# An encoder layer on one core: the issue order of the opening norms, weight splits and constant loads, and the place of the residual loads

## The chip, the core and the metric

The kernel runs on 1 core of one Trainium2 chip. Time is the device time of one execution in microseconds (us); the number compared is the median of several executions. The core has five engines that each take their own list of instructions strictly in order: TensorE (PE in the profile, its weight loads PEld), VectorE (DVE), ScalarE (ACT), GpSimd (POOL) and SyncE (SP). An instruction that waits holds back everything behind it on its engine. SyncE and GpSimd here also issue DMA transfers, which 16 DMA engines carry out.

## The reference, cut to what matters

One pre-norm layer over x of 2048 frames by 1024 channels, all in float32. The change touches the first step (the norm) and the residual addition.

```
h = rmsnorm(x, norm_mix)                  # x * rsqrt(mean(x*x) + 1e-6) * gain
proj = h @ w_in                           # columns: conv, S5, attention, HGRN groups
y = four mixers on the column groups, each rms-normalised with a gain
x = x + y @ w_out                         # residual
h = rmsnorm(x, norm_ffn)
x = x + square(relu(h @ w_ff1)) @ w_ff2
```

## The kernel before, in words

The 2048 frames go through the first half of the layer in 4 blocks of 512 (`TB`), each block in 4 tiles of 128 frames. Every matrix product is made of three float32r products: both operands are split into a high part (rounded) and a low part (the rest), and high*high, high*low and low*high are added in PSUM (`mm3`, L509 to L512).

**A norm** (`norm` in `make_hT`, L481 to L489) takes one tile: SyncE loads `xt` (512 KB, L484, 2 buffers); ScalarE squares it and adds up each row into `ssx` (L486); VectorE makes mean + eps (`rsx`, L92); GpSimd raises it to the power -0.5 (L93); VectorE multiplies the tile by it and by the gain `g_mix` (L488). TensorE then transposes the tile in two halves of four 128x128 blocks into the one PSUM buffer `tr` (L501), ScalarE writes the high part `hh` (L505) and VectorE the low part `hl` (L506). The second half's transposes wait until `hl` of the first half has read the buffer.

**A weight unit** (`load_split`, L98 to L111) is a 256 KB load into `wr` (L102, 6 buffers), a high part `wh` by ScalarE (L105) and a low part `wl` by VectorE (L111), 9 buffers each. The first product of the kernel (`attn_in`, through `tm_tile`, L531) needs 8 units and goes tile by tile: 24 matmuls a tile, into one of two PSUM buffers `mm`, which ScalarE (`qk`, L741) and VectorE (`va`, L742) empty. The products after it (`proj_fm`, L518) take two units each, starting with the 9th.

**Constants.** About 16 small loads are issued by GpSimd (L146 to L199: the masks `mraw`, `bones`, gains, `sink`, `lbp`, the GLU weights `wgr`), and VectorE turns them into what the mixers need (`masks` L147, `nsink` L172, `lbm` L179 and so on). Then come 11 loads for `s5_setup` (L229 to L244, from `lam` over `ldt` to `db`); the first VectorE instruction that needs one of these is L223, `t<-ldt`, on the table of time steps.

**The order.** The program text is handed to a scheduler that keeps the data dependences, sets buffers and waits, and orders each engine's list by priority: `first(-4000)` puts the norm of block 0 ahead of all, `tc.high_priority()` lifts the weight units. Which row stands first on an engine is therefore only seen in the built program. GpSimd's loads use 8 completion counters in turn, so that a load there waits for the one eight before it.

**The residual** (`outp`, L1101 to L1113) loops over two halves of the 1024 output columns and 4 tiles: a product with 8 units of `w_out`, a load `xr` of x (L1109, 2 buffers), `xr = product + xr` on VectorE (L1111), and a store to `x1d` (L1112). Beside it `out_in` (L1058 to L1098) transposes the operands of the next block through the same `tr` buffer.

## Time and profile before

| | us |
|---|---|
| median of 3 runs (2293.31 to 2297.61) | 2293.39 |
| the profiled execution, whole | 2296.33 |
| the same, span of its trace | 2294.5 |
| TensorE busy | 2205.3 |
| VectorE busy | 1449.5 |
| ScalarE busy | 961.3 |
| GpSimd busy | 194.4 |

The profiled execution lies 2.94 us above the median, and 1.83 us of it are outside the span. TensorE is busy for 96% of the span, so what can be won lies in the remaining 89 us: the places where TensorE has nothing to do. The views read are the busy time by stretch, TensorE's waits, and the list of instructions in order of time around the longest of them.

### The profile page before, as it was taken

Reading aid. Unit: us, or ns where it says so; the run is one execution under the profiler, and the core shown is the slowest. Engines: PE = TensorE matmul, PEld = TensorE weight load, DVE = VectorE, ACT = ScalarE, POOL = GpSimd, SP = SyncE. Lnnn points to the kernel's source line nnn. Section 1 sums busy time; section 2 is a strip of 40 time slices with the busy share of each in tenths; the row PEclk is TensorE's granted clock in tenths of the full one; section 3 lists DMA queues with packets and bytes.
Section 4 is the critical chain, followed back from the end, with each engine's and each line's share of the span. In section 5 each row is a group of like instructions: output and inputs, shape, how many; then the busy total and the mean of one; then the engine's idle time right before and its main releaser. Section 6 shows DMA issues by size and latency. Waiting matters only on the chain.

```text
span 2294.5 us, 32511 instructions
## 1 busy us (share of the span) xinstructions
PE 2205.3 (96%) x11460; PEld 1755.9 (77%) x11460; DVE 1449.5 (63%) x3044; ACT 961.3 (42%) x1914; POOL 194.4 (8%) x251
## 2 busy tenths in 40 slices
PE   4999999999999999999999999999999999999899
PEld 3777777777777787777788878888878877888787
DVE  4796796797679664596666676555534455465343
ACT  3444325324433433465565565555533223223121
POOL 3112212112211210000000000000000010000000
PEclk9999999999999999999999999999999999999999
DMA  6333334333443457646667575554655587475544
GB/s 174 97 89 94 98 98 138 109 105 100 139 116 104 129 195 232 196 153 202 195 196 210 151 235 156 152 148 147 201 165 195 181 293 233 146 248 175 190 165 152
DMA packets 391476, 372.97 MB, mean 163 GB/s; under 512 B 30656, under 2 KB 305184, under 8 KB 391312
## 3 DMA queue, kind: packets, MB, share of 16 engines
q1 hardware_dynamic: 388976, 365.05, 51.7%
q0 software_dynamic: 2336, 5.84, 1.0%
q8 instruction: 90, 1.47, 0.3%
q14 instruction: 74, 0.61, 0.1%
HBM read 265.97 MB, written 103.82 MB: 161 GB/s over the span
## 4 chain that ended last, share of the span: by engine, by line
PE 42%; DMA 6%; DVE 3%; ACT 1%; issue 1%; SPq 0%; DVEq 0%; ACTq 0%
PE mm L1548 19%; PE mm L1363 13%; PE hx L1363 7%; DMA wr<-in_w_ff_dram 5%; PE mx L1363 3%; DVE st L1520 1%; DMA tr<-tb 1%; DMA sr<-as 1%; DVE wr L1217 1%; DVE wl L1208 0%; ACT wh L1207 0%; ACT st L1519 0%; DMA tq<-x1d 0%; DVE tp L1217 0%; DVE tb L1327 0%
## 5 line engine op out<-in xcount | busy, mean ns | idle before, releaser
L1548 PE MATMUL mm<-wh,st 128*128 128x512 f32 x1728 | 549.2, 395 | 13.8 <-DVE tq L1217 6.1
L1548 PEld LDWEIGHTS mm<-wh,st 128*128 128x128 f32 x1728 | 325.8, 189 | 92.3 <-issue 9.6
L1548 PE MATMUL mm<-wl,st 128*128 128x512 f32 x864 | 341.1, 395 | 0.2 <-DVE wl L1208 0.2
L1363 PE MATMUL mm<-tb,wh 128*128 128x512 f32 x1024 | 323.8, 397 | 4.0 <-ACT tp L1369 1.9
L1519 ACT ACTIVATE st<-sr 128x1024 fp32r<-128x1024 f32 x112 | 115.4, 1054 | 343.6 <-PE mm L1548 244.2
L1363 PEld LDWEIGHTS mm<-tb,wh 128*128 128x128 f32 x1024 | 190.9, 189 | 53.7 <-ACT tp L1382 5.4
L510 PE MATMUL mm<-wh,hh 128*128 128x512 f32 x512 | 212.4, 415 | 0.7 <-ACT hh L505 0.7
L512 PE MATMUL mm<-wh,hl 128*128 128x512 f32 x512 | 205.9, 402 | 0.0
L105 ACT ACTIVATE wh<-wr 128x512 fp32r<-128x512 f32 x224 | 138.2, 629 | 158.6 <-PE mm L511 113.8
L511 PE MATMUL mm<-wl,hh 128*128 128x512 f32 x512 | 204.6, 400 | 0.0
L1363 PE MATMUL mm<-tb,wl 128*128 128x512 f32 x512 | 202.4, 396 | 1.0 <-DVE wl L1208 1.0
L1207 ACT ACTIVATE wh<-wr 128x512 fp32r<-128x512 f32 x204 | 124.8, 627 | 176.1 <-DVE wr L1217 83.4
L1548 PEld LDWEIGHTS mm<-wl,st 128*128 128x128 f32 x864 | 162.8, 188 | 38.9 <-DVE wl L1208 0.9
L1520 DVE TENSOR_TENSOR st<-sr,st 128x1024 fp32r<-128x1024 f32 x112 | 134.5, 1221 | 70.6 <-ACT st L1519 70.5
L111 DVE TENSOR_TENSOR wl<-wr,wh 128x512 fp32r<-128x512 f32 x224 | 150.2, 690 | 35.8 <-ACT wh L105 34.7
L1363 PE MATMUL hx<-tb,wh 128*128 128x512 f32 x512 | 161.1, 394 | 0.0
L1208 DVE TENSOR_TENSOR wl<-wr,wh 128x512 fp32r<-128x512 f32 x204 | 136.6, 687 | 36.5 <-ACT wh L1207 30.2
L510 PE MATMUL mm<-hh,wh 128*128 128x512 f32 x384 | 159.4, 415 | 0.0
L512 PE MATMUL mm<-hh,wl 128*128 128x512 f32 x384 | 152.7, 398 | 0.0
L511 PE MATMUL mm<-hl,wh 128*128 128x512 f32 x384 | 152.3, 397 | 0.0
L1363 PEld LDWEIGHTS mm<-tb,wl 128*128 128x128 f32 x512 | 96.6, 189 | 23.7 <-DVE wl L1208 1.4
L510 PEld LDWEIGHTS mm<-wh,hh 128*128 128x128 f32 x512 | 98.6, 193 | 20.8 <-ACT hh L505 1.3
(412 smaller groups left out, 3617.1 us busy)
## 6 DMA issues: line engine op xcount, KB each, us to landing
wr<-in_w_ff_dram SPq DMA_DIRECT2D x304, 256.0 KB, 3.9
as<-tp SPq DMA_DIRECT2D x224, 256.0 KB, 2.7
sr<-as SPq DMA_DIRECT2D x112, 512.0 KB, 4.6
wr<-in_w_in_dram SPq DMA_DIRECT2D x160, 256.0 KB, 3.1
wr<-in_w_out_dram SPq DMA_DIRECT2D x64, 256.0 KB, 4.0
xt<-in_x_dram SPq DMA_DIRECT2D x16, 512.0 KB, 3.6
xr<-in_x_dram SPq DMA_DIRECT2D x32, 256.0 KB, 3.0
x1d<-xr SPq DMA_DIRECT2D x32, 256.0 KB, 2.5
```

The source lines that it names most:

```text
L105: S.activation(out=hi, in_=raw, func=AF.Copy)
L111: (G if le == "p" else V).tensor_tensor(out=lo, in0=raw, in1=hi, op=ALU.subtract)
L510: PE.matmul(ps, lhsT=lh, rhs=rh, start=first, stop=False)
L511: PE.matmul(ps, lhsT=lh, rhs=rl, start=False, stop=False)
L512: PE.matmul(ps, lhsT=ll, rhs=rh, start=False, stop=last)
L1207: S.activation(out=h, in_=raw, func=AF.Copy)
L1208: V.tensor_tensor(out=l, in0=raw, in1=h, op=ALU.subtract)
L1217: V.tensor_tensor(out=o, in0=x, in1=y, op=op)
L1363: PE.matmul(ps, lhsT=(wh, wl)[lw][:, ks], rhs=b[lb][:, k, :], start=first and k == 0 and q == 0, stop=k == 3 and q == 2, skip_group_check= ...
L1519: S.activation(out=s_[:, 0, ks], in_=r, func=AF.Copy)
L1520: V.tensor_tensor(out=s_[:, 1, ks], in0=r, in1=s_[:, 0, ks], op=ALU.subtract)
L1548: PE.matmul(ps, lhsT=st_[:, ls, k, :], rhs=tu[n, k][lt], start=k == 0 and p_ == 0, stop=k == NJ - 1 and p_ == 2)
```

## The change

It has three parts. (1) `make_hT` and the gain's load move up in the text, and the norm of block 0 is written there; `rstd_of` keeps each GpSimd power in a list `pows`, and each norm keeps its power and its scaling. (2) With `tc.issue_after(...)`, everything written inside the block is put behind the given instruction: all constant loads and their arithmetic behind the first norm's power, the loads of `s5_setup` behind the fourth norm's power, and the first step of `attn_in` of block 0 (its 8 weight units and the first matmuls) behind the first norm's scaling. (3) In `outp` the load of `xr` is written ahead of the product and made high priority. No arithmetic is changed.

```
@@ -86,11 +86,13 @@
+    pows = []
     def rstd_of(pool, ss, n, inv, tag):
...
-        G.tensor_tensor(out=r, in0=r, in1=mhalf[:, 0:n], op=ALU.pow)
+        pows.append(G.tensor_tensor(out=r, in0=r, in1=mhalf[:, 0:n], op=ALU.pow).ins)
@@ -141,15 +143,62 @@
+    g_mix = c1.tile([P, D], F32, tag="gain", name="g_mix")
+    with first(-3998):
+        SY.dma_start(out=g_mix, in_=a["norm_mix"].partition_broadcast(P))
+    norms = []
+    def make_hT(b):
...
+            i_ = V.scalar_tensor_tensor(out=xt, in0=xt, scalar=r, in1=g_mix, op0=ALU.mult, op1=ALU.mult)
+            norms.append((pows[-1], i_.ins))
+            return xt
...
+    with first(-4000):
+        run(make_hT(0))
+    after = tc.issue_after(norms[0][0])
+    after.__enter__()
     masks = cm.tile([P, 4, P], U8, name="masks")
     mraw = mix.tile([P, 4, P], F32, tag="cva0", name="mraw")
     G.dma_start(out=mraw, in_=a["c_masks"])
...
@@ -200,6 +249,7 @@
         V.tensor_tensor(out=wgl[:, c], in0=wr, in1=wgh[:, c], op=ALU.subtract)
+    after.__exit__(None, None, None)
@@ -1103,20 +1122,15 @@
             for i in range(4):
-                ps = yield from tm_tile(ws, i)
                 xr = c1.tile([P, 512], F32, tag="xr", name="xr", bufs=2)
                 t0 = b * TB + i * P
-                SY.dma_start(out=xr, in_=a["x"][t0:t0 + P, ns])
+                with tc.high_priority():
+                    SY.dma_start(out=xr, in_=a["x"][t0:t0 + P, ns])
+                ps = yield from tm_tile(ws, i)
@@ -1147,13 +1161,16 @@
-    with first(-4000):
-        run(make_hT(0))
     s5p = None
     setup = s5_setup()
-    next(setup)
+    with tc.issue_after(norms[3][0]):
+        next(setup)
     for b in range(NB):
-        dense(attn_in(b))
+        g = attn_in(b)
+        if b == 0:
+            with tc.issue_after(norms[0][1]):
+                next(g)
+        dense(g)
```

The built programs differ in few rows: in the opening of all five engines, and around the residual on SyncE and VectorE. Line numbers in the rows of the changed kernel are its own.

**First norms.** VectorE, from its first row that waits for anything. Before:

```order
L147 CAST masks<-mraw 128x512
L92 TENSOR_SCALAR rsx<-ssx 128x1
L111 TENSOR_TENSOR wl<-wr,wh 128x512 x7
L488 SCALAR_TENSOR_TENSOR xt<-xt,rsx,g_mix 128x1024
L111 TENSOR_TENSOR wl<-wr,wh 128x512
L92 TENSOR_SCALAR rsx<-ssx 128x1
L111 TENSOR_TENSOR wl<-wr,wh 128x512
L488 SCALAR_TENSOR_TENSOR xt<-xt,rsx,g_mix 128x1024
L506 TENSOR_TENSOR hl<-tr,hh 128x4x128
```

Now:

```order
L94 TENSOR_SCALAR rsx<-ssx 128x1
L168 SCALAR_TENSOR_TENSOR xt<-xt,rsx,g_mix 128x1024
L94 TENSOR_SCALAR rsx<-ssx 128x1
L113 TENSOR_TENSOR wl<-wr,wh 128x512 x2
L168 SCALAR_TENSOR_TENSOR xt<-xt,rsx,g_mix 128x1024
L187 TENSOR_TENSOR hl<-tr,hh 128x4x128
L113 TENSOR_TENSOR wl<-wr,wh 128x512 x3
L187 TENSOR_TENSOR hl<-tr,hh 128x4x128
L113 TENSOR_TENSOR wl<-wr,wh 128x512 x3
L187 TENSOR_TENSOR hl<-tr,hh 128x4x128
```

The cast of the masks is gone from the head (it now stands behind the low part of the second tile's first half), the first scaling stands ahead of all weight splits, and the splits come in groups of 2, 3 and 3 between the norm's pieces.

GpSimd at the same place; `ISA` is a configuration instruction, the TENSOR_TENSOR rows are the norms' powers. Before (behind ten constant loads that begin with `mraw`):

```order
L168 DMA sink<-in_attn_sinks_dram 64x2x1
L93 ISA
L93 TENSOR_TENSOR rsx<-rsx,mhalf 128x1
L168 DMA sink<-in_attn_sinks_dram 64x2x1
L174 DMA ogain<-in_hg_out_norm_dram 128x64
L177 DMA lbp<-in_hg_lower_bounds_dram 128x2x1
L199 DMA wgr<-in_s_w_glu_dram 128x512
L93 TENSOR_TENSOR rsx<-rsx,mhalf 128x1
L199 DMA wgr<-in_s_w_glu_dram 128x512
L229 DMA lam<-in_s_lam_re_dram 8x128
```

Now, from the first row of the program proper:

```order
L95 ISA
L95 TENSOR_TENSOR rsx<-rsx,mhalf 128x1
L198 DMA mraw<-in_c_masks_dram 128x512
L201 DMA bones<-in_c_bones_dram 128x2
L203 DMA g_grp<-in_group_norm_dram 128x768
L95 TENSOR_TENSOR rsx<-rsx,mhalf 128x1
L205 DMA g_grpa<-in_group_norm_dram 128x2x1
```

The first power stands ahead of every load and the second behind three; the rest of the constants follow up to both `wgr`, then the third and the fourth power, and only then `lam` and the other loads of `s5_setup`.

**End of the opening.** VectorE around `t<-ldt`; `qss`, `qrs`, `qn` belong to the attention of the first tile. Before, with the third tile's `hl` as the last row:

```order
L742 COPY va<-mm 128x128
L223 TENSOR_SCALAR t_783<-ldt 128x8
L217 TENSOR_TENSOR db<-db,ident 16x256
L766 TENSOR_REDUCE qss<-qsq 128x6
L221 TENSOR_SCALAR t_784<-t_783 128x8
L92 TENSOR_SCALAR qrs<-qss 128x6
L221 TENSOR_SCALAR t_784<-t_784 128x8
L506 TENSOR_TENSOR hl<-tr,hh 128x4x128
```

Now, ending with the `va` of the third tile, which frees a PSUM buffer:

```order
L789 TENSOR_TENSOR qn<-qk,qrs 128x2x2x64
L187 TENSOR_TENSOR hl<-tr,hh 128x4x128
L793 TENSOR_TENSOR qn<-qk,qrs 128x128
L168 SCALAR_TENSOR_TENSOR xt<-xt,rsx,g_mix 128x1024
L273 TENSOR_SCALAR t_783<-ldt 128x8
L267 TENSOR_TENSOR db<-db,ident 16x256
L271 TENSOR_SCALAR t_784<-t_783 128x8
L271 TENSOR_SCALAR t_784<-t_784 128x8
L761 COPY va<-mm 128x128
```

All eight `hl` of block 0 now stand ahead of `t<-ldt` (the last of them is seen here), and behind it come the third tile's `va` and, further on, the low parts of the weight units from the 10th.

**Residual.** SyncE in the second block's turn; `x1d` rows are the stores, `w_out` rows the weight units of the next half. Before:

```order
L1109 DMA xr<-in_x_dram 128x512
L1112 DMA x1d_64<-xr 128x512
L102 DMA wr<-in_w_out_dram 128x512 x8
L1112 DMA x1d_64<-xr 128x512
L1109 DMA xr<-in_x_dram 128x512 x2
L1112 DMA x1d_64<-xr 128x512
L1071 DMA ybt<-ybd_76 128x256
L1072 DMA ybt<-ycdd_79 128x512
L1109 DMA xr<-in_x_dram 128x512
```

Now:

```order
L1128 DMA xr<-in_x_dram 128x512
L1132 DMA x1d_64<-xr 128x512
L104 DMA wr<-in_w_out_dram 128x512 x3
L1128 DMA xr<-in_x_dram 128x512
L104 DMA wr<-in_w_out_dram 128x512 x5
L1132 DMA x1d_64<-xr 128x512 x2
L1128 DMA xr<-in_x_dram 128x512 x2
```

The first `xr` of the new half stands behind three of the eight weight loads instead of behind all eight. The same is found in the third block's turn, and in the first block's with three of six.

## Rows read from the trace of the kernel before

**Rows 1.** The page: the span, the busy times of the engines with their share and instruction count, the group of VectorE's weight splits (busy in all, mean ns of one, idle before), and two DMA groups over the whole span (count, KB each, median us from issue to landing).

```profile
span 2294.5 us, 32511 instructions
...
PE 2205.3 (96%) x11460; PEld 1755.9 (77%) x11460; DVE 1449.5 (63%) x3044; ACT 961.3 (42%) x1914; POOL 194.4 (8%) x251
...
L111 DVE TENSOR_TENSOR wl<-wr,wh 128x512 fp32r<-128x512 f32 x224 | 150.2, 690 | 35.8 <-ACT wh L105 34.7
...
xr<-in_x_dram SPq DMA_DIRECT2D x32, 256.0 KB, 3.0
x1d<-xr SPq DMA_DIRECT2D x32, 256.0 KB, 2.5
```

**Rows 2.** Busy time by stretch, late in the opening and behind it: from:to, length, then PE, PEld, DVE, ACT and POOL busy (instructions), granted clock of TensorE, DMA share, GB/s.

```profile
40.00:60.00 20.00, 15.34 (x66) 12.63 (x67) 11.82 (x36) 8.51 (x16) 2.98 (x4) 0.83 0.24 82
60.00:100.00 40.00, 40.00 (x213) 32.14 (x212) 25.75 (x69) 16.62 (x45) 7.04 (x6) 1.00 0.44 122
```

**Rows 3.** TensorE's waits over the whole span: who waited for whom, us in all, times, the longest.

```profile
PE tr L501 <- DVE xt L488: 21.9, 1, 21.9
PE tr L501 <- DVE hl L506: 8.5, 3, 7.6
PE tr L1093 <- DVE hl L1098: 6.8, 4, 3.0
```

**Rows 4.** Instructions in order of time, from the first constant load to the end of the first tile: start, duration, engine, line, what, and the idle time before it with its releaser.

```profile
1.26 0.68 POOL L146 DMA_DIRECT2D mraw<-in_c_masks_dram  x1 [0.81 <-POOLq L1578]
...
1.67 0.42 SPq L152 DMA_DIRECT2D g_mix<-in_norm_mix_dram  x1
...
4.32 1.06 ACT L486 ACTIVATE junk<-xt 128x1024 bf16<-128x1024 f32 x1 [2.30 <-DMA xt<-in_x_dram]
...
7.37 0.43 DVE L147 CAST masks<-mraw 128x512 uint8<-128x512 f32 x1 [5.76 <-DMA mraw<-in_c_masks_dram]
...
10.62 0.60 POOL L168 DMA_DIRECT2D sink<-in_attn_sinks_dram  x1 [1.95 <-DMA g_grp<-in_group_norm_dram]
11.33 0.59 POOL L93 TENSOR_TENSOR rsx<-rsx,mhalf 128x1 f32<-128x1 f32 x1
...
13.06 0.72 POOL L177 DMA_DIRECT2D lbp<-in_hg_lower_bounds_dram  x1
...
14.56 2.43 ACT L105 ACTIVATE wh<-wr 128x512 fp32r<-128x512 f32 x4 [1.22 <-DMA wr<-in_w_in_dram]
...
20.56 1.28 DVE L488 SCALAR_TENSOR_TENSOR xt<-xt,rsx,g_mix 128x1024 f32<-128x1024 f32 x1
...
21.75 0.68 DVE L111 TENSOR_TENSOR wl<-wr,wh 128x512 fp32r<-128x512 f32 x1
...
21.89 1.11 PE L501 MATMUL tr<-ident,xt 128*128 128x128 f32 x4 [21.89 <-DVE xt L488]
...
33.53 0.49 ACT L741 ACTIVATE qk<-mm 128x384 f32<-128x384 f32 x1 [0.79 <-PE mm L512]
```

**Rows 5.** DMA issues of the first 60 us: count, KB each, median us from issue to landing.

```profile
xt<-in_x_dram SPq DMA_DIRECT2D x6, 512.0 KB, 3.6
g_mix<-in_norm_mix_dram SPq DMA_DIRECT2D x1, 512.0 KB, 7.7
...
lbp<-in_hg_lower_bounds_dram POOLq DMA_DIRECT2D x1, 1.0 KB, 5.0
```

**Rows 6.** In order of time: GpSimd's issue of the first load of the S5 setup and of the two loads of `ldt`, and SyncE's issue of the fourth tile.

```profile
24.07 0.55 POOL L229 DMA_DIRECT2D lam<-in_s_lam_re_dram  x1
...
29.81 1.39 POOL L240 DMA_DIRECT2D ldt<-in_s_log_dt_dram  x2
...
32.14 0.33 SPq L484 DMA_DIRECT2D xt<-in_x_dram  x1
```

**Rows 7.** In order of time: VectorE's first instruction on `ldt`, what stands around it, and TensorE up to the first product behind `attn_in`.

```profile
42.71 0.17 DVE L223 TENSOR_SCALAR t<-ldt 128x8 f32<-128x8 f32 x1 [7.81 <-DMA ldt<-in_s_log_dt_dram]
...
43.94 1.06 ACT L486 ACTIVATE junk<-xt 128x1024 bf16<-128x1024 f32 x1 [7.89 <-DMA xt<-in_x_dram]
...
44.66 1.11 PE L501 MATMUL tr<-ident,xt 128*128 128x128 f32 x4 [7.62 <-DVE hl L506]
...
61.80 0.39 PE L510 MATMUL mm<-hh,wh 128*128 128x512 f32 x1
```

**Rows 8.** In order of time: SyncE, VectorE and TensorE around the first `xr` of the second half in the second block's turn.

```profile
869.76 0.32 SPq L1112 DMA_DIRECT2D x1d<-xr  x1
...
870.74 5.67 SPq L102 DMA_DIRECT2D wr<-in_w_out_dram  x8
...
876.93 4.23 SPq L1109 DMA_DIRECT2D xr<-in_x_dram  x2
...
881.53 0.69 DVE L1111 TENSOR_TENSOR xr<-mm,xr 128x512 f32<-128x512 f32 x1 [5.15 <-DMA xr<-in_x_dram]
...
882.75 0.55 PE L1093 MATMUL tr<-ident,ybt 128*128 128x128 f32 x3 [2.98 <-DVE hl L1098]
```

**Rows 9.** The same in the third block's turn.

```profile
930.29 0.69 DVE L1111 TENSOR_TENSOR xr<-mm,xr 128x512 f32<-128x512 f32 x1 [5.20 <-DMA xr<-in_x_dram]
...
931.50 0.55 PE L1093 MATMUL tr<-ident,ybt 128*128 128x128 f32 x3 [2.00 <-DVE hl L1098]
```

**Rows 10.** Busy time of the 8 us behind that, in the columns of rows 2.

```profile
932.00:940.00 8.00, 8.00 (x36) 6.46 (x34) 2.30 (x5) 1.74 (x5) 0.00 (x0) 0.79 0.41 140
```

More of the change, by code (lines that the diff above doesn't have):

```diff
@@ L143, in emit, with run, norm @@
     junks = {k: cm.tile([P, GW], BF16, name="junk" + k) for k in "chg"}
+    g_mix = c1.tile([P, D], F32, tag="gain", name="g_mix")
+    with first(-3998):
+        SY.dma_start(out=g_mix, in_=a["norm_mix"].partition_broadcast(P))
+    def run(g):
+        r = None
+        for r in g:
+            pass
+        return r
+    norms = []
+    def make_hT(b):
+        def norm(i):
+            t0 = b * TB + i * P
+            xt = big.tile([P, D], F32, tag="xt", name="xt", bufs=2)
+            SY.dma_start(out=xt, in_=a["x"][t0:t0 + P, :])
+            ss = mix.tile([P, 1], F32, tag="ssx", name="ssx", bufs=2)
+            S.activation(out=junk, in_=xt, func=AF.Square, accum_out=ss)
+            r = rstd_of(mix, ss, 1, 1.0 / D, "rsx")
+            i_ = V.scalar_tensor_tensor(out=xt, in0=xt, scalar=r, in1=g_mix, op0=ALU.mult, op1=ALU.mult)
+            norms.append((pows[-1], i_.ins))
+            return xt
+        nx = norm(0)
+        yield
+        for i in range(4):
+            xt = nx
+            if i < 3:
+                nx = norm(i + 1)
+            for k4 in range(2):
+                pt = psum_tr()
+                for k in range(4):
+                    kk = k4 * 4 + k
+                    PE.transpose(pt[:, k * P:(k + 1) * P], xt[:, kk * P:(kk + 1) * P], ident)
+                pv = pt.rearrange("p (k t) -> p k t", k=4)
+                oh = hh[:, k4 * 4:k4 * 4 + 4, i * P:(i + 1) * P]
+                ol = hl[:, k4 * 4:k4 * 4 + 4, i * P:(i + 1) * P]
+                S.activation(out=oh, in_=pv, func=AF.Copy)
+                V.tensor_tensor(out=ol, in0=pv, in1=oh, op=ALU.subtract)
+                yield
+    with first(-4000):
+        run(make_hT(0))
+    after = tc.issue_after(norms[0][0])
+    after.__enter__()
     masks = cm.tile([P, 4, P], U8, name="masks")
@@ L149, in emit @@
     G.dma_start(out=bones, in_=a["c_bones"])
-    g_mix = c1.tile([P, D], F32, tag="gain", name="g_mix")
-    with first(-3998):
-        SY.dma_start(out=g_mix, in_=a["norm_mix"].partition_broadcast(P))
     g_grp = cm.tile([P, 3 * GW], F32, name="g_grp")
@@ L475, in s5_setup @@
                 SY.dma_start(out=two_d[:, gp, 2:4, :], in_=wsb)
-                yield
-    def make_hT(b):
-        def norm(i):
-            t0 = b * TB + i * P
-            xt = big.tile([P, D], F32, tag="xt", name="xt", bufs=2)
-            SY.dma_start(out=xt, in_=a["x"][t0:t0 + P, :])
-            ss = mix.tile([P, 1], F32, tag="ssx", name="ssx", bufs=2)
-            S.activation(out=junk, in_=xt, func=AF.Square, accum_out=ss)
-            r = rstd_of(mix, ss, 1, 1.0 / D, "rsx")
-            V.scalar_tensor_tensor(out=xt, in0=xt, scalar=r, in1=g_mix, op0=ALU.mult, op1=ALU.mult)
-            return xt
-        nx = norm(0)
-        yield
-        for i in range(4):
-            xt = nx
-            if i < 3:
-                nx = norm(i + 1)
-            for k4 in range(2):
-                pt = psum_tr()
-                for k in range(4):
-                    kk = k4 * 4 + k
-                    PE.transpose(pt[:, k * P:(k + 1) * P], xt[:, kk * P:(kk + 1) * P], ident)
-                pv = pt.rearrange("p (k t) -> p k t", k=4)
-                oh = hh[:, k4 * 4:k4 * 4 + 4, i * P:(i + 1) * P]
-                ol = hl[:, k4 * 4:k4 * 4 + 4, i * P:(i + 1) * P]
-                S.activation(out=oh, in_=pv, func=AF.Copy)
-                V.tensor_tensor(out=ol, in0=pv, in1=oh, op=ALU.subtract)
                 yield
@@ L1113, in outp @@
                 yield True
-    def run(g):
-        r = None
-        for r in g:
-            pass
-        return r
     tracks = []
```

## The prediction

> **What bounds the kernel now.** TensorE is busy for 2205.3 of 2294.5 us [rows 1]. An edit that only reorders work can win from the 89 us in which it stands, so the first view to read is TensorE's waits. One wait leads it by far: 21.9 us at the start, for the first scaled tile. Two more lie where the change reaches: 8.5 us in three waits for a norm's low part, one of them 7.6 us, and 6.8 us in four waits for the low part in `out_in` [rows 3]. The second view is the order of time around each, and there the question is what the engine that is named was itself waiting for.
>
> At the start VectorE holds the tile back, but not because it has work. The squares are done at 5.4 us; VectorE then stands at the cast of the masks until that load has landed, at 7.37. GpSimd, which has to raise to a power, is issuing constant loads and waits for one of them until 10.62; its power runs at 11.33 and is done at 11.9. By then VectorE stands in front of seven weight splits, and the first weights are not there before 14.56. The scaling runs at 20.56, the first transposes at 21.89, and the first tile is done at 33.53 [rows 4]. So two queues, not two computations, cost about 13 us.
>
> At 42.71 the same happens again: VectorE waits 7.81 us for `ldt`, a load of the S5 setup that nobody needs yet, and the third tile's low part is behind it; TensorE waits 7.62 us for that and starts at 44.66. The fourth tile, issued at 32.14, is there only at 43.94, 11.8 us later where 3.6 is the median [rows 5 to 7]; the two loads of `ldt` were moving in between. The first product behind `attn_in` begins at 61.80 [rows 7], and from there TensorE has no gap: 40.00 of 40 us [rows 2]. That makes 61.80 the mark to measure the opening by: what comes earlier there comes earlier at the end, since behind it the lists of all engines are the same up to the residual.
>
> **The change part by part: the first norm.** Removed from the path: the cast and the wait for its load, and the ten loads ahead of the power. The squares end at 5.4; two small steps, VectorE's (0.17, as in rows 7) and GpSimd's 0.59, give 6.3. The scaling also needs the gain: issued at 1.67, 7.7 to land, that is 9.4 [rows 4, 5]. That was with 640 KB of masks and gains on the same DMA engines; a 512 KB tile alone took 3.6, so the bounds are 6.3 and 9.4. I take 7.5, since the constants now come behind. Scaling 1.28: the first transposes at about 8.9 instead of 21.89. This is no gain of 13 us by itself, because the first tile's products need all eight weight units. Before, the eighth split ran at 21.75 [rows 4]; its loads are two buffers ahead at most, so I leave it at 20 to 22. The first tile is then done at about 22.5 instead of 33.5: eleven us at this point.
>
> The first power carries a risk that a page names: the Trainium skill, GPSIMD Engine Reference, section Instruction dispatch, says that the first call to a freshly loaded GpSimd kernel pays an instruction load of about 6 us that no row shows. The trace speaks against it: the first power ran at 11.33, 0.11 us after the load issue in front of it ended. By that page the sum would be some 6 us smaller in the opening; it is a rival below.
>
> **The third and fourth norm: what is late next.** The constants moved behind the first power. VectorE now has `nsink` and `lbm`, which need `sink` and `lbp`, ahead of the third scaling. Before, `lbp` was issued at 13.06 and took 5.0: landed at 18.1, 16.8 us after the first constant was issued at 1.26 [rows 4, 5]. The same train now starts at 6.4, so `lbp` lands at 23.2. Without it the third scaling could run at about 20.6 (transposes of the first tile done at 15, load 3.6, square 1.2, power 0.7). I take 23.3; the bounds are 20.6 and 28, the latter if the train is slowed by 5 us by the weights it now shares the engines with.
>
> From there VectorE's list up to the fourth norm's power holds the scaling (1.28), five full-width steps (0.69 each, the mean of the weight splits [rows 1]: 3.45), two halvings of the GLU weights (estimate 0.5 each, half the operands of a split) and about eight small ones (0.17: 1.4), 7.1 us; the power 0.6. So `lam`, the first load of the S5 setup, is issued at 31 instead of 24.07 [rows 6], with bounds 28 and 36. From `lam` to `ldt` landed it was 18.6 us (24.07 to 42.71) [rows 6, 7]: GpSimd's issue of eleven loads and the slow `ldt` itself, both unchanged. **So `ldt` lands at 49.6**, 7 us later than before.
>
> What waits for it has changed. All low parts of block 0 are now ahead of it. TensorE gets the fourth tile at about 32 to 33.4, has some two tiles of products left (24 matmuls each, about 5 us by the 213 in 40 us of rows 2) and is through at about 45. Then it needs a PSUM buffer, and the `va` that frees it is behind `ldt` on VectorE: 49.6 and four short steps, 50.8. The mark thus moves from 61.80 to 50.8: 11.0 us earlier. Two things come off. The second half of that product needs the tenth unit's low part, which has nine small steps (1.5), a norm's steps (0.2, 0.6, 1.28) and itself (0.69) ahead of it: 55.0, where TensorE arrives at 53.3; with VectorE's steps overlapping I take 1.5. And the pause of 6 us lies ahead of dense work: behind the pause of 7.6 the granted clock of the stretch was 0.83 [rows 2], so 3.4 of 20 us were lost at the lower level; about 1 us more than before. **Opening: -11.0 + 1.5 + 1.0 = -8.5 us**, bounds -3.5 (`lam` at 36) and -12 (`lam` at 28, no clock loss).
>
> **The residual loads.** In the second block's turn VectorE stood 5.15 us at the residual addition, from 876.4 to 881.53, for an `xr` issued at 876.93 behind eight weight loads, and the low part for TensorE was behind it: TensorE waited 2.98 [rows 8]. In the third block's turn it was 5.20 and 2.00 [rows 9]. Now `xr` goes out behind three of the eight: at 870.74 plus three eighths of 5.67, 872.9. Its buffer was stored from 869.76, 2.5 to land: free at 872.3. It takes 3.0 to 4.6 and is there at 876 to 877.5; VectorE then reaches the low part as soon as ScalarE's high part is there. Both of TensorE's waits go: **-5.0 us**. Bounds: -1, if another wait of VectorE takes the place; -6.7, since behind the second one the clock was 0.79 for 8 us [rows 10], 1.7 us lost. The other loads that move by one or two rows cost nothing: two 256 KB issues of 0.4 us each, in front of weights that VectorE paces.
>
> **Sum.** -8.5 - 5.0 = -13.5. On the profiled execution 2296.3 becomes 2282.8; it lay 2.9 above the median, and 2293.4 becomes **2279.9**, say 2280.0.
>
> **The rivals.** *The residual loads bring nothing* (VectorE waits for the product or a weight split there instead; against it: its wait was for the DMA alone, and TensorE's product was done): -8.5, 2285.0. Chance 0.13. *The first power pays a start cost of its own*, by the rule of the page cited: constants, `lam` and `ldt` 6 us later, opening -2.5, in all -7.5, 2286. Against it the 0.11 us. Chance 0.08. *The S5 loads take back the opening*: the third norm's constants, or the eight counters of GpSimd's loads, hold the fourth power until `lam` goes out at 38 to 40; then `ldt` lands at 57 to 59, the mark is at 59 to 61, and what is left is about half of the residual's gain: 2291, no change. For it: each of these loads took 5 us and more when weights ran beside it. Chance 0.11. *Slower: an `xr` load holds the weights.* It stands in the middle of `w_out` loads, and SyncE waits there until the buffer is free. If that buffer is the one stored at 876.46 and not at 869.76, five weight loads are held until about 879, 6 us in each of three turns, and TensorE needs them in the next half: +18 against -8.5, 2303. It decides itself by whether SyncE idles over 2 us behind the third weight load. Against it: before, the first `xr` went out right behind the store issue, with no wait. Chance 0.08.
>
> **How the numbers follow.** My forecast has 0.55, a larger gain (under 2272, if `ldt` is no longer the last to come) 0.05. About 0.2% of this kernel, 4.6 us, can be told from no change: faster is under 2288.8. Faster: 0.55 + 0.05 + 0.13 + 0.08 = 0.81; same 0.11; slower 0.08. The forecast's own bounds are 2274.7 to 2288.9. The range leaves out the slower rival, half of the no-change one and the larger gain, under 2 in 10: 2272.0 to 2290.0.
>
> **What would show it.** First transposes at 8 to 11 us; first tile done at 20 to 24; `lam` issued at 28 to 36; VectorE waiting for `ldt` with the low parts ahead of it, until 47 to 55; the first product behind `attn_in` at 49 to 58; in the residual no wait of VectorE for `xr` over 1 us and TensorE's wait for the `out_in` low part down from 6.8 to about 2. I am wrong if a constant that I let land by 23 is there only after 30, or if a later wait grows by what the opening wins: TensorE's waits behind 61.80 must stay what they are.

## The result, and the profile after

| | us |
|---|---|
| before, on the same chip: median of 4 runs (2293.31 to 2297.61) | 2294.63 |
| after: median of 4 runs (2280.79 to 2284.63) | 2281.13 |
| ratio after to before, with its 95% interval | 0.9943 (0.9927 to 0.9959) |
| profiled execution of after, span | 2282.9 |

The change makes the kernel 0.57% faster: 13.1 us by the ratio, where 13.5 were forecast. Line numbers below are those of the changed kernel, unless a row of before is named.

The first views are the page and TensorE's waits over the span; they answer to [rows 1] and [rows 3].

```profile
span 2282.9 us, 32514 instructions
...
PE 2205.5 (97%) x11460; PEld 1755.1 (77%) x11460; DVE 1447.6 (63%) x3044; ACT 959.6 (42%) x1914; POOL 194.7 (9%) x251
```

```profile
PE tr L182 <- DVE xt L168: 8.4, 1, 8.4
...
PE tr L182 <- DVE hl L187: 6.4, 2, 6.0
...
PE mm L529 <- DVE va L761: 4.2, 1, 4.2
```

TensorE's busy time is that of before to 0.2 us; the gain is idle time alone. The wait for the first scaled tile fell from 21.9 to 8.4 us, and the wait for a low part from 8.5 to 6.4. A new one stands where the prediction put it: 4.2 us for `va`, behind `ldt`.

The opening in order of time, which answers to [rows 4, 6, 7]: start, duration, engine, line, what, and the idle time ahead with its releaser.

```profile
5.80 0.56 POOL L95 TENSOR_TENSOR rsx<-rsx,mhalf 128x1 f32<-128x1 f32 x1 [5.35 <-DVE rsx L94]
7.09 1.28 DVE L168 SCALAR_TENSOR_TENSOR xt<-xt,rsx,g_mix 128x1024 f32<-128x1024 f32 x1 [1.38 <-DMA g_mix<-in_norm_mix_dram]
8.43 1.11 PE L182 MATMUL tr<-ident,xt 128*128 128x128 f32 x4 [8.43 <-DVE xt L168]
16.58 0.71 POOL L226 DMA_DIRECT2D lbp<-in_hg_lower_bounds_dram  x1
25.85 0.16 DVE L228 TENSOR_TENSOR lbm<-lbp 128x2 f32<-128x2 f32 x1 [4.02 <-DMA lbp<-in_hg_lower_bounds_dram]
25.93 1.28 DVE L168 SCALAR_TENSOR_TENSOR xt<-xt,rsx,g_mix 128x1024 f32<-128x1024 f32 x1
26.63 0.48 ACT L760 ACTIVATE qk<-mm 128x384 f32<-128x384 f32 x1
32.53 0.58 POOL L279 DMA_DIRECT2D lam<-in_s_lam_re_dram  x1
38.24 1.38 POOL L290 DMA_DIRECT2D ldt<-in_s_log_dt_dram  x2
38.80 0.34 SPq L164 DMA_DIRECT2D xt<-in_x_dram  x1
47.45 1.06 ACT L166 ACTIVATE junk<-xt 128x1024 bf16<-128x1024 f32 x1 [5.20 <-DMA xt<-in_x_dram]
50.38 0.17 DVE L273 TENSOR_SCALAR t<-ldt 128x8 f32<-128x8 f32 x1 [6.37 <-DMA ldt<-in_s_log_dt_dram]
51.08 0.28 DVE L761 COPY va<-mm 128x128 f32<-128x128 f32 x1
51.41 0.80 PE L529 MATMUL mm<-hh,wh 128*128 128x512 f32 x1 [4.25 <-DVE va L761]
```

The chain of the prediction is all there: the third scaling stands behind `lbp`, `lam` behind the fourth norm's power, the first product behind `attn_in` (the mark) behind `ldt` and `va`. The mark went from 61.80 to 51.41.

The residual in the second block's turn, which answers to [rows 8]:

```profile
861.46 1.53 SPq L104 DMA_DIRECT2D wr<-in_w_out_dram  x3
863.08 0.38 SPq L1128 DMA_DIRECT2D xr<-in_x_dram  x1
863.56 3.71 SPq L104 DMA_DIRECT2D wr<-in_w_out_dram  x5
867.31 3.28 SPq L1132 DMA_DIRECT2D x1d<-xr  x2
873.37 0.95 SPq L1128 DMA_DIRECT2D xr<-in_x_dram  x2
```

```profile
864.36 0.69 DVE L1131 TENSOR_TENSOR xr<-mm,xr 128x512 f32<-128x512 f32 x1
869.55 0.69 DVE L1131 TENSOR_TENSOR xr<-mm,xr 128x512 f32<-128x512 f32 x1 [2.30 <-PE mm L530]
...
876.13 0.69 DVE L1131 TENSOR_TENSOR xr<-mm,xr 128x512 f32<-128x512 f32 x1 [3.67 <-DMA xr<-in_x_dram]
...
900.02 0.69 DVE L1131 TENSOR_TENSOR xr<-mm,xr 128x512 f32<-128x512 f32 x1 [4.72 <-DMA xr<-in_x_dram]
```

The first `xr` of the half is in time now (869.55 waits for the product alone). The second is not: the sum of 864.36 is stored only at 867.31, behind five weight loads, and its buffer is the one that the second `xr` needs, so that goes out at 873.37. VectorE still waits 8.4 us in two for `xr` between 780 and 1010 us, where it was 10.6 in three before. The store of 867.31 went out 2.3 us behind its sum (864.36 and 0.69) and landed only at 873.35, 6.0 us later, where the median over the span is 3.3; most of the delay is thus the landing beside the weight loads and not the place in the queue. But TensorE hardly feels the new place: of the 2.98 us of [rows 8] this is left, and nothing of the 2.00 of [rows 9].

```profile
881.76 0.55 PE L1112 MATMUL tr<-ident,ybt 128*128 128x128 f32 x3 [1.12 <-DVE hl L1117]
```

**Where the time is won along the program.** Each number is a difference worked out from two traces: the start of the k-th execution of a line on ScalarE or VectorE, less that of the same execution before, and of these the median over a stretch (us of the kernel before). Each row is one profile; the two profiles of the change differ by 1.5 to 2.0 us, so a smaller difference between rows says nothing.

| kernel | 70 to 100 | 800 to 850 | 1000 to 1020 |
|---|---|---|---|
| after | -8.1 | -9.4 | -11.9 |
| after, profiled again | -6.5 | -7.4 | -13.4 |
| opening alone | -7.1 | -5.7 | -7.4 |
| residual loads alone | +0.1 | +0.6 | -4.6 |
| S5 loads a norm earlier | -5.6 | -5.4 | -11.3 |
| `ldt` as rows | -14.4 | -10.5 | -15.8 |
| `sink`, `lbp` first | -10.7 | -11.9 | -17.8 |
| constants at the head | -5.6 | -5.2 | -9.2 |
| store early | -7.7 | -5.2 | -7.6 |
| store by GpSimd | -7.3 | -5.7 | -12.2 |
| before with `ldt` as rows | -6.5 | -6.8 | -7.6 |
| both edits of the opening | -18.7 | -13.3 | -20.4 |

### The profile page after: what moved, and what is told of

It is laid out like the page before. It is cut to its first block, busy times and chain, and to the rows that moved or that the text cites. A ratio compares the mean times of both kernels' runs of the same rounds, so it can differ in the third digit from the quotient of the medians.

```text
span 2282.9 us, 32514 instructions
## 1 busy us (share of the span) xinstructions
PE 2205.5 (97%) x11460; PEld 1755.1 (77%) x11460; DVE 1447.6 (63%) x3044; ACT 959.6 (42%) x1914; POOL 194.7 (9%) x251
## 4 chain that ended last, share of the span: by engine, by line
issue 32%; PE 16%; DMA 3%; DVE 1%; POOL 0%; ACT 0%; SPq 0%; POOLq 0%; DVEq 0%; ACTq 0%
PE mm L1565 13%; DMA wr<-in_w_ff_dram 2%; PE mm L1380 2%; PE hx L1380 1%; DMA fxs<-x1d 0%; POOL tt L1523 0%; DVE tp L1234 0%; DVE st L1537 0%; PE mx L1380 0%; DVE wl L1225 0%; DVE wr L1234 0%; ACT wh L1224 0%; DMA tq<-x1d 0%; DMA tt<-wr 0%; SPq L1329 0%
## 5 line engine op out<-in xcount | busy, mean ns | idle before, releaser
L1565 PE MATMUL mm<-wh,st 128*128 128x512 f32 x1728 | 549.8, 396 | 14.4 <-DVE tq L1234 7.2
```

The source lines that it names most:

```text
L1565: PE.matmul(ps, lhsT=st_[:, ls, k, :], rhs=tu[n, k][lt], start=k == 0 and p_ == 0, stop=k == NJ - 1 and p_ == 2)
```

## The experiments

Differences in us are the ratio less one, times the median of the kernel before on the same chip (2295.57, 2293.71 and 2293.70). A kernel's own median stands ahead of its ratio.

**The parts by themselves.** The first kernel is after with this put back:

```
-                with tc.high_priority():
-                    SY.dma_start(out=xr, in_=a["x"][t0:t0 + P, ns])
                 ps = yield from tm_tile(ws, i)
+                SY.dma_start(out=xr, in_=a["x"][t0:t0 + P, ns])
```

> The kernel after, with the residual loads where they were before (the load of xr written behind the product, without priority). My theory (opening and residual gain separately, the opening carries most): TensorE's mark, the first product behind attn_in, stays at 51.4 as in the kernel after; between 930 and 950 us the shift against the kernel before stays at the opening's -9.2 instead of the -14.0 of the kernel after, the 5.15 and 5.20 us waits of VectorE for xr are back, and the time is about 2285 (9.2 below 2294.6), so 3 to 4 us above the kernel after. Rival (the residual loads bring nothing by the end, since the lists behind give the gain back): the same shift at the end, -11.7, and a time within 1 us of the kernel after, 2281.

2287.29, ratio 0.9963 (0.9949 to 0.9978): -8.5 us. The interval overlaps with that of the change (0.9927 to 0.9959), so the time alone does not tell the two apart. The waits are back, VectorE's for `xr` (5.65 and 5.02 us) and TensorE's for the low part (3.6).

The second is before with the residual change alone:

> The kernel before, with the residual change alone (the load of xr ahead of the product, high priority); the opening is as before. My theory: the mark is at 61.8 as before, the first xr of a half no longer holds VectorE, the second one does for 3 to 4 us because SyncE holds two stores until its buffer's sum is there; the shift against the kernel before is 0 up to 840 us, about -5 at 930 to 950 and -2.5 behind 1000, the time 2292, 2.5 below the kernel before. The prediction's own term: -5.0, 2289.6. Rival (nothing): 2294.6.

2291.25, ratio 0.9988 (0.9975 to 1.0001): -2.8 us, at the edge of what can be told from nothing. VectorE still waits 11.0 us in three for `xr`; TensorE's wait for the low part between 855 and 935 us is down from 5.0 to 0.8. So by these two times the opening carries about three quarters of the change (-8.5 beside -2.8). That the residual loads are worth something is not shown by the time, whose interval includes nothing, but by the shift along the program: -5.2 from 800 to 1010 us here, -0.8 and -1.7 in the two kernels without that change.

After itself, beside the others:

> The kernel after itself, to stand beside the others on the same chip: 0.9943 of the kernel before, about 2281 to 2283.

2281.93, ratio 0.9950 (0.9931 to 0.9968): -11.5 us. Its mark is at 52.74; over the five runs with this opening it lies between 51.37 and 52.96. Part of that spread is another load: between `ldt` and `va` VectorE's list has a step on `db`, and in this profile it waits 1.16 us for that.

**What sets the end of the opening.** The S5 loads one norm earlier:

```
-    with tc.issue_after(norms[3][0]):
+    with tc.issue_after(norms[2][0]):
         next(setup)
```

> The kernel after, with the loads of the S5 setup behind the third norm's power instead of the fourth's. My theory (ldt is what sets the mark, and its time is counted from the issue of lam): lam goes out at about 21 to 25 instead of 32.5, t<-ldt is ready at 40 to 43 instead of 50.38, and the mark is then set by the fourth tile's products, which end at 47.1: mark 47 to 48, time 3 to 4 us below the kernel after (2277.5). Rival (GpSimd's eleven load issues stand ahead of the fourth power and the slow ldt holds the fourth tile's load): the fourth scaling slips by 5 us or more, the mark stays at 51 or later, time the same or up to 5 us longer.

2287.38, ratio 0.9958 (0.9943 to 0.9973): -9.6 us. The rival had the mark right, but not the way: the fourth scaling did not slip, it runs at 32.96 (32.60 in the change). `lam` went out at 21.59 and `ldt` was there at 43.05, but the fourth tile's first low part (the seventh of eight `hl`, at 44.31) is now behind it on VectorE, and TensorE waits 6.25 us for that. The fifth tile, the first of the next block, was issued at 33.34 and could be squared only at 45.99:

```profile
43.05 0.17 DVE L273 TENSOR_SCALAR t<-ldt 128x8 f32<-128x8 f32 x1 [6.28 <-DMA ldt<-in_s_log_dt_dram]
...
45.05 1.12 PE L182 MATMUL tr<-ident,xt 128*128 128x128 f32 x4 [6.25 <-DVE hl L187]
...
45.99 1.06 ACT L166 ACTIVATE junk<-xt 128x1024 bf16<-128x1024 f32 x1 [8.18 <-DMA xt<-in_x_dram]
```

The mark is at 56.25, 3.3 to 4.9 us behind that of the change. The time (0.9958 beside 0.9943 and 0.9950 for the change) does not tell them apart. It is the old picture of [rows 7], two low parts later.

The loads of `ldt` in another form:

```
-            for g2 in range(2):
-                G.dma_start(out=ldt[g2 * 64:(g2 + 1) * 64, :],
-                             in_=a["s5_log_dt"].rearrange("(q g) -> g q", g=2)[g2].partition_broadcast(64), ...)
+            lrow = st.tile([P, 16], F32, name="lrow")
+            G.dma_start(out=lrow, in_=a["s5_log_dt"].partition_broadcast(P))
...
+            for g2 in range(2):
+                V.tensor_copy(out=ldt[g2 * 64:(g2 + 1) * 64, :],
+                              in_=lrow[g2 * 64:(g2 + 1) * 64].rearrange("p (q g) -> p q g", g=2)[:, :, g2])
             exp_acc(dt, ldt)
```

> The kernel after, with the time steps of the S5 setup loaded otherwise: one contiguous row of 16 numbers broadcast to 128 partitions and two small VectorE copies, in place of two loads that pick single 4-byte numbers for 64 partitions each. What is computed is the same. My theory (the two loads themselves are slow, 8 us and more, and hold other transfers): the row lands within 4 us of its issue, about 43 to 44, the fourth tile's load is down from 11.8 us towards the usual 3.6, t<-ldt no longer waits or waits under 2 us, the mark goes from 51.4 to 47 to 48, the time 3 to 4 us below the kernel after (2277.5). Rival (the slowness is that of GpSimd's queue and of the loads ahead of ldt, not of its form): ldt lands at 49 to 50 as now, mark and time the same as the kernel after, 2281.

2278.97, ratio 0.9919 (0.9903 to 0.9936): -18.6 us. In order of time:

```profile
38.73 0.56 POOL L290 DMA_DIRECT2D lrow<-in_s_log_dt_dram  x1
38.84 0.33 SPq L164 DMA_DIRECT2D xt<-in_x_dram  x1
...
43.68 1.06 ACT L166 ACTIVATE junk<-xt 128x1024 bf16<-128x1024 f32 x1 [1.36 <-DMA xt<-in_x_dram]
43.76 0.34 DVE L333 COPY ldt<-lrow 64x8 f32<-64x8 f32 x2 [1.23 <-DMA lrow<-in_s_log_dt_dram]
...
47.07 0.39 PE L530 MATMUL mm<-hh,wh 128*128 128x512 f32 x1
```

The tile that SyncE issues at 38.84 is squared at 43.68; in the kernel after, issued at 38.80, at 47.45. It is the sixth tile, the second of the next block, and not the fourth: in the kernel after, the fourth is issued at 20.28 and squared at 30.55, so what `ldt` held there was not a tile that the mark needs. The mark is at 47.07, right behind the last product of the four tiles, and `va` is no longer waited for. For the mark the theory holds, and the time fell by more than its 3 to 4 us; the intervals of this run and of the change just overlap (0.9936 and 0.9927), so it is the mark and the waits that decide.

The same in the kernel before:

> The kernel before, with the time steps of the S5 setup loaded as one contiguous row broadcast to 128 partitions and two small copies, as in the run on the kernel after. My theory (the two strided loads hold the other queues as well, and this cost stands in both kernels): t<-ldt runs by 36 instead of 42.71, the fourth tile's load takes 4 to 5 us instead of 11.8, TensorE's 7.62 us wait for the third tile's low part falls under 2, and the mark goes from 61.80 to 54 to 56; time 6 to 7 us below the kernel before. Rival (VectorE's and GpSimd's order around it sets the mark): mark 60 or later, time within 2 us of the kernel before.

2289.66, ratio 0.9978 (0.9962 to 0.9994): -5.0 us. `t<-ldt` runs at 34.00, the 7.62 us wait of [rows 7] is 0.93, the mark is at 55.33. So the two strided loads cost both kernels: 5.0 us here, 5.5 to 7.1 in the kernel after (-18.6 beside -13.1 and -11.5). With rows in both, the change still wins 13.6 us (-18.6 beside -5.0), so its gain is not one of going around them; by the mark it is somewhat less, 8.3 us (55.33 to 47.07) instead of 10.4.

**The constants.** `sink` and `lbp` first in their train; the lines are taken out at their old places:

```
     after = tc.issue_after(norms[0][0])
     after.__enter__()
+    sink = cm.tile([P, 2], F32, name="sink")
+    for r in range(2):
+        G.dma_start(out=sink[r * 64:(r + 1) * 64, :], ...)
+    lbp = cm.tile([P, 2], F32, name="lbp")
+    G.dma_start(out=lbp, in_=a["hg_lower_bounds"].rearrange("(c p) -> p c", p=P), ...)
     masks = cm.tile([P, 4, P], U8, name="masks")
```

> The kernel after, with the loads of sink and lbp first in the train of constants instead of tenth to thirteenth. My theory (the third scaling, 25.9 us in the kernel after, stands behind nsink and lbm, which wait 1.36 and 4.02 us for these two loads): lbp is there before 15 us, the third scaling runs at 21.7 to 22.5, right behind the third power (21.06 and 0.56), TensorE's 6.0 us wait for the low part falls to about 2, lam goes out at 28 to 29 and the mark comes with it from 51.4 to 47 to 48; time 4 us below the kernel after. Rival (the third scaling then waits for something else, the masks or the weights; or ldt is held by the weight loads and keeps its place): mark 50 to 52, time within 1.5 us of the kernel after.

2280.37, ratio 0.9936 (0.9917 to 0.9955): -14.7 us. The third scaling runs at 22.25, behind its power and nothing else, and `lam` goes out at 29.96; `ldt` follows it in the old distance:

```profile
22.25 1.28 DVE L168 SCALAR_TENSOR_TENSOR xt<-xt,rsx,g_mix 128x1024 f32<-128x1024 f32 x1 [0.59 <-POOL rsx L95]
...
29.96 0.57 POOL L279 DMA_DIRECT2D lam<-in_s_lam_re_dram  x1
...
47.78 0.17 DVE L273 TENSOR_SCALAR t<-ldt 128x8 f32<-128x8 f32 x1 [6.34 <-DMA ldt<-in_s_log_dt_dram]
```

The mark is at 48.82, 2.6 us ahead of the change's, behind the 47 to 48 expected by the 1 us that `lam` is late; the time (0.9936 beside 0.9943 and 0.9950) does not tell the two apart.

The constants back at the head (the hold behind the first power taken out, the rest of the change kept):

```
-    after = tc.issue_after(norms[0][0])
-    after.__enter__()
...
-    after.__exit__(None, None, None)
```

> The kernel after, with the constant loads at the head again (not behind the first norm's power); the rest of the change stays. This leaves the cast of the masks and ten load issues ahead of the first power. My theory (the first tile is paced by the eighth weight unit and not by the first scaling, and the constants behind the power are what holds the third scaling): first transposes at 12.5 to 13.5 instead of 8.43, first tile done within 1 us of the kernel after, lbp there at about 18 to 19 instead of 25.85, third scaling at 22 to 23, lam at 28 to 29, the mark 47 to 49; time 2 to 4 us below the kernel after. Rival (my prediction's view that this hold is where the opening's gain comes from): the constant loads slow the gain and the weights, the first tile is done 4 us or more later, the mark at 54 to 56, time 3 to 5 us above the kernel after.

2286.62, ratio 0.9959 (0.9945 to 0.9973): -9.4 us, which cannot be told from the change run again (0.9950). Neither theory holds. `lbp` is there in time, as I thought, but the first scaling at 11.74 puts all of the first two tiles later, the third tile is issued at 19.75 instead of 14.36, and its scaling comes at 25.71, hardly sooner than behind `lbp`. `lam` goes out at 31.59 and `t<-ldt` runs at 49.41, 0.8 to 2.5 us earlier than in the five kernels with the hold. All the same the mark is at 53.63, 0.7 to 2.3 us behind theirs:

```profile
49.41 0.17 DVE L270 TENSOR_SCALAR t<-ldt 128x8 f32<-128x8 f32 x1 [6.95 <-DMA ldt<-in_s_log_dt_dram]
...
52.09 1.28 DVE L168 SCALAR_TENSOR_TENSOR xt<-xt,rsx,g_mix 128x1024 f32<-128x1024 f32 x1 [0.46 <-POOL rsx L95]
53.30 0.28 DVE L758 COPY va<-mm 128x128 f32<-128x128 f32 x1
```

In the change `va` runs 0.70 us behind `t<-ldt` (50.38 and 51.08). Here VectorE's list came out otherwise: ten more small steps and the scaling of a tile of the next block stand between them, 3.89 us. So the later mark is an effect of that order, and not of the time at which the constants land.

**The residual's second wait.** The store made high priority as well:

```
-                SY.dma_start(out=x1_d[b][i * P:(i + 1) * P, ns], in_=xr)
+                with tc.high_priority():
+                    SY.dma_start(out=x1_d[b][i * P:(i + 1) * P, ns], in_=xr)
```

> The kernel after, with the store of the residual sum high priority too, so that SyncE issues it ahead of the last weight loads of the half and not behind them. My theory (in the kernel after the second xr of the second half goes out only at 873.37, because the sum of 864.36 is stored at 867.31, behind five weight loads, and its buffer is that xr's): the store goes out at about 865 to 866, the xr by 870, VectorE's wait of 3.67 us at 876.13 and the next one of 4.72 fall under 1 us each, TensorE's 1.1 goes; the shift against the kernel before at 962 to 1010 us goes from -12 to -13 or -14, time 1 to 2 us below the kernel after. Rival one (two buffers are too few whatever the order): xr waits as before, time the same. Rival two (the store now waits for the sum in front of weight loads, and these come late): TensorE waits for weights in the next half, time 2 to 5 us longer.

2289.55, ratio 0.9980 (0.9968 to 0.9992): -4.6 us, 7 us slower than the change on the same chip. The order came out as the second rival had it, the price another way. VectorE's waits for `xr` fall to 2.7 us in one, but SyncE stands at each store until its sum is there, with weight loads behind it:

```profile
862.50 0.33 SPq L1128 DMA_DIRECT2D xr<-in_x_dram  x1
864.84 0.32 SPq L1133 DMA_DIRECT2D x1d<-xr  x1
865.94 1.53 SPq L104 DMA_DIRECT2D wr<-in_w_out_dram  x3
```

The first weights of the half go out at 865.94 instead of 861.46. But TensorE has no wait for weights between 840 and 1030 us; its one long wait there is 2.91 us for a low part at 887.36, whose high part stands on ScalarE behind a wait of 5.38 us for a load of the next norm (`tp`). About 3 us of the residual's gain are missing at 1000 us, and more is lost behind it; what loses it there was not followed up.

The store on another queue:

```
-                SY.dma_start(out=x1_d[b][i * P:(i + 1) * P, ns], in_=xr)
+                G.dma_start(out=x1_d[b][i * P:(i + 1) * P, ns], in_=xr)
```

> The kernel after, with the stores of the residual sum issued by GpSimd instead of SyncE; SyncE's other rows keep their order. My theory (the second xr of a half is late because the store that frees its buffer stands behind five weight loads on SyncE, and not because two buffers are too few): the store of the sum of 864.36 goes out within 1 us of the sum, the second xr by 870, VectorE's waits of 3.67 and 4.72 us for xr fall under 1 us each, TensorE's wait of 1.1 us goes, and the shift against the kernel before at 962 to 1010 us grows by 1 to 3 us over that of the kernel after; time 1 to 3 us below it. Rival (two buffers are too few whatever the order of issue, or the loads themselves are slow beside eight weight loads): the waits stay over 3 us each and the time is the same.

2288.36, ratio 0.9966 (0.9950 to 0.9982): -7.8 us. In its place the theory holds for the waits: VectorE never waits for `xr`, and TensorE has no wait for the low part; the transposes come every 3.09 us. It does not hold for the second `xr`, expected by 870: the store goes out at 868.92, 0.3 us behind its sum, and takes 5.6 us to land, so `xr` goes out at 874.58. The loads and stores are slow beside eight weight loads, as the rival said.

```profile
876.99 0.49 PE L1112 MATMUL tr<-ident,ybt 128*128 128x128 f32 x3
880.08 0.49 PE L1112 MATMUL tr<-ident,ybt 128*128 128x128 f32 x3
...
886.26 0.49 PE L1112 MATMUL tr<-ident,ybt 128*128 128x128 f32 x3
```

But the shift through the residual (from 800 to 1010 us in the table) is -6.5 us, and it is -2.5 and -6.0 in the two profiles of the change and -7.1 with both edits of the opening: what VectorE's 8 to 11 us of waiting were worth lies inside that spread. The expectation was wrong in one more thing: SyncE's other rows did not all keep their order. The loads of the next stage's norm moved, and between 1050 and 1200 us 6 us of the shift are lost: TensorE waits 3.6 us for ScalarE's `tp` (a tile of that norm), and the granted clock is 0.91 from 1060 to 1080. That the moved loads are the cause is not shown. Whether a third `xr` buffer would do better was not run.

**Both edits of the opening**, the `ldt` rows and the moved `sink` and `lbp` together:

> The kernel after with both edits of the opening: sink and lbp first in the train of constants, and the time steps as one contiguous row. My theory (the third scaling and then ldt are the two waits in line; each alone leaves the other): third scaling at 22.3, lam at 30, no wait for ldt, mark at 43 to 44 (47.07 with the row alone, less the 3.7 us that the scaling comes earlier), TensorE without a gap over 1 us from 25 on; time 7 to 8 us below the kernel after, about 2274. Rival (the weights behind attn_in or the fourth tile are late then): mark 47, time 2278 to 2279.

2274.11, ratio 0.9898 (0.9874 to 0.9921): -23.4 us. Third scaling at 22.01, `lam` at 29.79, mark at 42.78, and TensorE is busy for 19.97 of the 20 us from 40 at full clock, where [rows 2] had 15.34 and 0.83:

```profile
40.00:60.00 20.00, 19.97 (x89) 15.82 (x89) 16.32 (x47) 9.89 (x22) 1.88 (x2) 1.00 0.55 151
```

This is the lowest ratio of the kernels run here. Its interval lies below that of the change, and overlaps with that of the `ldt` rows alone (0.9903 to 0.9936).

The same with the store by GpSimd:

> The same with the residual's stores on GpSimd. If both theories hold, the two gains add: 8 to 10 us below the kernel after, about 2272. Rival: as e45_both, 2274.

2277.20, ratio 0.9913 (0.9884 to 0.9942): -20.0 us, no gain over the two edits. The rival was right.

## Why the prediction was right, point by point

**The first norm.** 8.43 for the first transposes, where 8.9 was forecast. The scaling waits 1.38 us for `g_mix`, which needed 5.3 us to land and not 7.7: the middle between the bounds was right. The first power began 0.24 us after the start of the step that makes its input (5.56, 0.15 us long) and took 0.56, so the start cost of about 6 us that the Trainium skill, GPSIMD Engine Reference, section Instruction dispatch, gives for a freshly loaded kernel is not in this trace; that rival falls.

**The first tile** was done at 26.63, not 22.5, by its `qk`. The prediction had the eighth weight split pace it, at 20 to 22; that split ran at about 17, and TensorE's products for the tile ended at 21.9 without a wait for weights. TensorE had been idle since 21.9 (it waits 5.97 us, until 27.87); ScalarE stood 5.42 us at its step on `lbm`, which needs `lbp`, with `qk` behind it. This sign missed because I let VectorE alone stand behind the constants. It cost nothing, as the next transposes waited for the same load.

**Third scaling to mark.** Forecast 23.3, 31, 49.6, 50.8 for third scaling, `lam`, `ldt` and mark; measured 25.93, 32.53, 50.38, 51.41. The term that is off is `lbp`: it took 9.2 us to land instead of 5.0, of which 1.5 came back because it was issued sooner (10.3 us behind the first constant instead of 11.8); the third scaling stayed inside its bounds. From `lam` to `t<-ldt` it was 17.85 us (18.64 before), 17.59 to 18.21 in the experiments with the strided loads behind the fourth power, and 21.46 in the one with them behind the third, where GpSimd twice waited for an earlier load to land before it could issue the next.

**What comes off the mark.** Forecast 1.5 us for the tenth unit's low part and 1.0 for the clock. The wait did not come, and the clock took all of it: TensorE's stretch behind the pause ran at its lower level of 1.2 GHz.

```profile
51.00:56.00 5.00, 4.59 (x11) 3.66 (x12) 4.41 (x16) 1.09 (x3) 0.55 (x1) 0.50 0.06 13
```

4.59 us at half speed lose 2.3; the shift goes from -10.4 at the mark to -8.1 behind it. The sum of the two, 2.5, held for a reason that was half wrong, which is luck. **Opening:** forecast -8.5; -8.5 in the run of the opening alone (-11.7 to -5.0 by its interval); along the program, over the five profiles with it, -6.5 to -8.1 at 70 to 100 us and -5.2 to -9.4 at 800 to 850.

**What in the change carries it** was not asked in the prediction. The hold of the constants does not: with them at the head the mark is still 8.2 us ahead of before's (53.63 and 61.80), `ldt` was there even earlier than with the hold, and the 0.7 to 2.3 us that the mark lost went to the place of `va`. The S5 loads behind the fourth power and not the third are worth 3.3 to 4.9 us at the mark, by that run. What is left would belong to the norm's place ahead of the weight splits and to the low parts ahead of `ldt`; these were not run apart, so that share is argued and not shown. The hold on the first step of `attn_in` moves no row: the program built without it has the same lists on all five engines.

**The residual.** Forecast -5.0; -2.8 in the run of it alone, -3.0 to -4.6 as the difference of change and opening alone, and about -4 along the program (from 800 to 1010 us the eight profiles with it and with the store as before average -5.2, the two without it -1.3). Here the step failed that said how: "in the residual no wait of VectorE for `xr` over 1 us". VectorE waits nearly as long as before (10.6 us): 8.4 and 10.0 in the two profiles of the change, 6.2 to 11.2 in the others with it. I followed the first `xr` of the half and not the second, whose buffer is freed by a store that SyncE issues behind the five weight loads; and I let a store land in 2.5 us, where this one took 6.0 beside them. TensorE's wait for the low part went all the same, from 6.8 to 3.0 us over the span, since the wait now falls where TensorE has products in hand. The term was mis-sized by some 1 to 2 us, as far as these readings can tell.

**The sum.** That 13.1 came out so near 13.5 is partly luck: the same kernel run again gave -11.5, and the parts run alone add up to -11.3. The prediction also named a sign of being wrong: TensorE's waits behind the mark must stay what they are. Summed from the traces, TensorE's idle time ahead of the mark falls by 10.0 us (31.1 to 21.1, and 21.2 in the change's second profile) and behind it by 1.7 (58.1 to 56.3, and 54.6). Single waits there moved both ways, such as 6.1 to 7.2 us for `tq` and 2.5 to 3.1 for the low part at L1281; none grew by what the opening won.

**The rivals.** In the half shown no `xr` held the weights: SyncE issued it 0.1 us behind the third (862.99, 863.08). Ahead of the half after it, one `xr` stood 2.05 us for its buffer, with seven weight loads behind it (884.75, 886.80), and TensorE had no wait for weights from it between 855 and 935 us. The S5 loads did not take the opening back; put one norm earlier, they took back 3 to 5 us of it at the mark.

## What to carry to other kernels

Follow a load that nobody needs yet to the engine that waits for it in program order, and ask what stands behind that wait; then look at the form of the load before moving it. A buffer is free when its store has landed, so a prefetch has to be followed back to the place of that store in its queue, and to what moves beside it: the same store landed in 2.0 us ahead of the weight loads (the run with the store early) and in 6.0 behind them. A run that moves one thing can reorder another, so look at the list in front of the mark before giving the mark a cause. And a wait of a helper engine is worth only what the bounding engine sees of it: most of VectorE's 10.6 us stayed, and more than half of TensorE's 6.8 went.

## What the runs showed of the hardware

**A load of 4-byte pieces holds the DMA engines.** In the kernel after, while `ldt` (2 loads of 2 KB) is under way: the stretch of 3 us from 40, in the columns of [rows 2] with the share of the 16 DMA engines and GB/s last, first in the kernel after, then with `ldt` as rows.

```profile
40.00:43.00 3.00, 3.00 (x15) 2.49 (x14) 1.42 (x4) 0.49 (x1) 2.06 (x3) 1.00 1.08 12
```

```profile
40.00:43.00 3.00, 3.00 (x15) 2.45 (x14) 1.29 (x4) 0.49 (x1) 1.75 (x2) 1.00 0.58 184
```

The share adds up the time of all packets that began in the stretch, so it can pass 1. The DMA engines are at work in both; they move 12 GB/s with the strided loads and 184 without. By queue, from 40 to 46 us of the kernel after (packets, MB, share of the engines' time), `software_dynamic` being GpSimd's:

```profile
q0 software_dynamic: 39, 0.01, 77.4%
q1 hardware_dynamic: 118, 0.44, 18.4%
```

Some 7 KB (0.01 MB) take 77.4% of the engines, and a 512 KB tile of another queue waits: 8.7 us from its issue at 38.80 to its square, 4.8 with `ldt` as rows. The next load on GpSimd's queue, `db`, took 10.8 us and takes 4.6. The packets in the trace show where the time is: the two loads of `ldt` are 32 packets of 128 bytes, and each took 2.1 to 3.6 us; a 4 KB packet of the tile took 0.16 us, and the 16 packets of 512 bytes of the row form at most 0.32.

**In one stretch the clock gives part of an early gain back.** With both edits the shift is -18.7 us at 70 to 100 and -13.3 at 800. About 3 of these 5.4 us go between 280 and 300 us of its trace (the shift is -16.8 ahead of it and -13.7 behind), where no wait is new: TensorE is busy for 18.68 of 20 us there as in the kernel after, but at a granted clock of 0.83 and not 1.00, which is 3.4 us lost. First with both edits, then in the kernel after:

```profile
280.00:300.00 20.00, 18.68 (x103) 13.34 (x99) 16.34 (x39) 5.54 (x14) 2.72 (x3) 0.83 0.28 77
```

```profile
280.00:300.00 20.00, 18.68 (x140) 13.77 (x140) 19.56 (x51) 4.33 (x9) 4.70 (x4) 1.00 0.24 70
```

Why the clock falls there in this kernel and with `ldt` as rows (0.83 too, and 0.91 with both edits and the store by GpSimd), and not in the change, stays open.
